# First two unit pairs multiply a split x, the norm factor moves to the eviction, and the taps are dealt out anew: conv and retention trunk on one core

## The chip, the core and the metric

The kernel runs on one core of a Trainium2 chip. The metric is the time of one execution on the device in microseconds (us). All products are made on TensorE (PE); VectorE (DVE), ScalarE (ACT) and GpSimd (POOL) do the elementwise work, SyncE (SP) issues most of the loads.

## The reference, cut to what matters

Sequence 512, model width 1024, inner width 2048, float32, two layers and a last norm:

```python
h = rms_norm(x, conv_norm)                  # x * r * g, r = 1/sqrt(mean(x^2) + eps) for each token
a, b, z = split(h @ w_in, 3)                # w_in: 1024 x 6144
u = a * sigmoid(b)
c = causal_depthwise_conv(u, 31 taps) + dw_b
y = silu(layer_norm(c)) * silu(z)
x = x + y @ w_out
x = x + retention(rms_norm(x, ret_norm))    # q, k, v, gate projections, rotary, chunks of 128
out = rms_norm(x, final_norm)
```

r is one number for each token, so (x * g * r) @ w is ((x * g) @ w) * r: the factor can be put in before the products or at their eviction.

## The kernel before, in words

Everything is held with channels on the 128 partitions and the 512 tokens along the free axis. x is 8 tiles of 128x512, u and c are 16 tiles each. Weights come from HBM in 64 pairs of units; a unit is 128x1024, which is 8 blocks of 128x128 for one output tile (two units make one u tile: unit 2j gives a, unit 2j+1 gives b).

Where a product has to be exact to float32, both factors are split into a high part (rounded to the type fp32r) and the rest, and three products are added: `mm3` (L231 to L235) does hi*hi, hi*lo, lo*hi. One unit is 24 such products. The pair 0 is the exception: `raw0` and `xg` (x times the norm's weight) are unsplit float32 and are multiplied in one pass each at L328 (16 products, for which the trace shows two records each).

**The start.** Ten products of zeros keep TensorE warm (`keep_warm`, L133). x and pair 0 are loaded, ACT squares each x tile (L295), DVE sums them up (L299), a product with ones gives the token sums (L288), `rsqrt` on DVE gives r (L250 to L267), and a product with the identity spreads it over the partitions as R1 (L273), in the middle of the products of pair 0. Then `h_tile` (L671) makes h = xg * R1 in PSUM (L674), ACT rounds it to its high part (L675), and `h_lo` (L677) makes the rest on DVE. `split_pair` (L681) splits pairs 1 and 2, with the low part on POOL. Pair 1 is multiplied at L735 to L742, first with all high parts of the weights, then with the low ones; its products wait for the h tiles one by one. From unit 4 on `unit_mm` (L745) runs one unit after the other. Here the high and low parts come from ACT (L198, L202: 1.9 us for a pair each) and from a DMA that POOL issues and that adds raw onto the negated high part (`dma_lo`, L204).

**The taps.** A u tile takes 31 taps of 128x512 for its c tile, 496 taps in all. Four ways take them: the first tap of a tile on ACT (`first_tap`, L373), a tap on DVE (L521: c = u shifted * w + c, in PSUM), a tap as a product on ACT and an add on POOL (`product` L432, `pool_add` L441), and a pair step: two products of tiles 2n and 2n+1 on ACT, added by one DMA of 512 KB that POOL issues (`pair_step` L408, `pair_add` L422).

**What sets the order.** From the start of this stage to the end of the layer norm the order on each engine is written out by hand (manual schedule): a planner in the kernel keeps a clock with five lines (`Clock`, L77) and in `fill` (L554) always emits the step that can start first. `pool_tile` (L536) picks the tile for POOL's next add: the tile next to be taken up by DVE or the one behind it, up to `POOL_CAP` taps, and not the first if `RATE` says that it would be late. `pair_of` (L397) lets a pair take a pair step if both its u tiles exist, none of its adds waits on POOL, it has done fewer than `STEPS`, its tiles lie behind the one next to be taken up, and one of two sum buffers is free (`room`, L393). Between pair steps the planner lets the DMA land and then 7 us pass (`QWAIT`), so an add that follows is put some 10.1 us (1.55 + 1.46 + 0.1 + 7.0) behind the DMA's issue. Only the pairs in `PAIRS` are asked.

```python
STEPS = 4
PAIRS = (2, 3, 4, 5)
...
        p = n // 2 + 1 + n % 2
...
            neg_hi(p)
            fill(it.done[f"wneg{p}"])
            dma_lo(p)
...
        prev = (prev or ()) + (unit_mm(n),)
        fill(it.now[PE_])
```

**The end of the stage.** Units 46 and 47 are held back (`HOLD`, L794); `work` (L800) puts their products, three at a time, between the products of the layer norm's sums (`tail`, L828), and where they have run out, products of zeros into `idle` (L811). Then follow the norm's factors, y and the output projection (L936 to L959), and the retention layer, whose order the scheduler sets.

## Time and profile before

| | us |
|---|---|
| median of 3 runs | 805.14 (802.46 to 807.92) |
| the profiled execution | 804.36 |
| its span, first to last instruction | 802.4 |
| mean granted TensorE clock | 0.993 |

The profile is of one execution; the span leaves out 2.0 us around it. A row of a timeline gives the start, the time from its start to its end (for several instructions merged, from the first start to the last end), the engine, the line of the kernel, the operation, what it writes and reads, and in brackets how long the engine had been idle before it and what ended that. An instruction begins before the one ahead of it has ended, so a merged row divided by its count is the step from one to the next.

### The profile page before, as it was taken

The page shows a single profiled execution, that of the slowest core. Times are in us where ns is not written, and L with a number is a line of the kernel's source. Part 1 is how long each engine was busy: PE and PEld are TensorE (multiplying, and loading weights), DVE is VectorE, ACT ScalarE, POOL GpSimd, SP SyncE. Part 2 cuts the span into 40 slices and gives each one's busy share as a digit, 9 for nine tenths or more (in the row PEclk, how much of TensorE's full clock was granted, in tenths as well). Part 3 has the DMA queues.
Part 4 walks back from the last instruction along what each step waited for, and adds up shares of the span by engine and source line. Part 5 has one row for each costly group of instructions (what it writes and reads, how often), then busy time and mean ns, then how long its engine had stood idle before and what let it go on. Part 6 is the DMA issues. An engine that isn't in the chain of part 4 may idle for free.

```text
span 802.4 us, 9733 instructions
## 1 busy us (share of the span) xinstructions
PE 789.1 (98%) x3681; PEld 651.7 (81%) x3681; DVE 576.8 (72%) x855; ACT 422.2 (53%) x561; POOL 365.8 (46%) x286
## 2 busy tenths in 40 slices
PE   8999999999999999999999999999999999999995
PEld 3588888888888888888888888888888888888895
DVE  4899999999999948899574576486586467542434
ACT  3589889888998727543233413423424424332421
POOL 0578999989999848720330322340340120000300
PEclk9999999999999999999999999999999999999998
DMA  7367857897798734433213212112122212222103
GB/s 276 124 174 176 210 164 167 211 238 176 199 232 214 182 108 145 171 105 106 105 54 128 81 53 105 53 54 105 52 69 96 99 53 105 105 105 105 53 1 105
DMA packets 18958, 101.58 MB, mean 127 GB/s; under 512 B 2272, under 2 KB 4320, under 8 KB 8032
## 3 DMA queue, kind: packets, MB, share of 16 engines
q1 hardware_dynamic: 14448, 74.73, 26.6%
q0 software_dynamic: 4032, 25.69, 15.8%
q8 instruction: 29, 0.48, 0.2%
q10 hardware_dynamic: 432, 0.54, 0.2%
q14 instruction: 17, 0.14, 0.0%
HBM read 73.17 MB, written 2.10 MB: 94 GB/s over the span
## 4 chain that ended last, share of the span: by engine, by line
PE 95%; DVE 2%; DMA 2%; ACT 1%; issue 0%; SPq 0%; DVEq 0%; ACTq 0%
PE mm L233 28%; PE mm L235 27%; PE mm L234 27%; PE mm L959 2%; PE mm L957 2%; PE mm L958 2%; DMA g<-xT 1%; PE dsum L288 1%; PE mm L328 1%; PE st L288 1%; PE acc L235 1%; PE acc L234 1%; PE acc L233 1%; PE mm L742 0%; PE st L647 0%; DMA nrm<-norms 0%
## 5 line engine op out<-in xcount | busy, mean ns | idle before, releaser
L233 PE MATMUL mm<-g,whi 128*128 128x512 f32 (+1 forms) x832 | 319.8, 385 | 0.0
L234 PE MATMUL mm<-g,whi 128*128 128x512 f32 (+1 forms) x832 | 317.5, 382 | 0.0
L235 PE MATMUL mm<-g,wlo 128*128 128x512 f32 (+1 forms) x832 | 316.8, 381 | 0.0
L521 DVE SCALAR_TENSOR_TENSOR acc<-u,cpar,acc 128x512 f32<-128x512 f32 x324 | 220.8, 753 | 4.7 <-ACT acc L473 3.0
L299 POOL TENSOR_TENSOR accp<-accp,prod 128x512 f32<-128x512 f32 x142 | 190.6, 1383 | 17.2 <-ACT prod L436 10.7
L233 PEld LDWEIGHTS mm<-g,whi 128*128 128x128 f32 x832 | 156.5, 188 | 30.3 <-issue 0.7
L234 PEld LDWEIGHTS mm<-g,whi 128*128 128x128 f32 x832 | 156.5, 188 | 30.1 <-issue 1.0
L235 PEld LDWEIGHTS mm<-g,wlo 128*128 128x128 f32 x832 | 156.4, 188 | 29.9
L187 ACT CAST whi<-raw 128x1024 fp32r<-128x1024 f32 x80 | 80.7, 1050 | 111.3 <-PE mm L234 69.2
L192 DVE TENSOR_TENSOR wlo<-raw,whi 128x1024 fp32r<-128x1024 f32 x70 | 94.5, 1384 | 41.3 <-ACT whi L187 41.3
L299 POOL TENSOR_TENSOR g<-g,g 128x512 f32<-128x512 f32 x23 | 35.5, 1544 | 179.9 <-ACT g L295 171.4
L436 ACT ACTIVATE prod<-u,cpar 128x512 f32<-128x512 f32 x142 | 97.3, 719 | 20.1 <-POOL accp L299 20.0
L1045 POOL TENSOR_TENSOR g<-g,g 128x512 f32<-128x512 f32 x8 | 10.4, 1294 | 142.7 <-DVE g L1043 142.7
L228 DVE TENSOR_TENSOR g<-g,g 128x512 fp32r<-128x512 f32 x36 | 29.0, 820 | 35.7 <-ACT g L227 32.2
L227 ACT CAST g<-g 128x512 fp32r<-128x512 f32 x36 | 22.4, 623 | 60.0 <-POOL g L1045 27.8
L234 PE MATMUL mm<-wlo,g 128*128 128x512 f32 x128 | 49.8, 389 | 0.0
L235 PE MATMUL mm<-whi,g 128*128 128x512 f32 x128 | 49.6, 389 | 0.0
L233 PE MATMUL mm<-whi,g 128*128 128x512 f32 x128 | 49.3, 389 | 0.0
L198 ACT ACTIVATE wlo<-raw 128x2048 fp32r<-128x2048 f32 x21 | 40.1, 1909 | 0.0
L202 ACT CAST whi<-raw 128x2048 fp32r<-128x2048 f32 x21 | 40.0, 1904 | 0.0
L1112 POOL TENSOR_TENSOR o<-o,g 128x512 f32<-128x512 f32 x16 | 27.5, 1747 | 18.2 <-DVE g L267 18.2
L192 POOL TENSOR_TENSOR wlo<-raw,whi 128x1024 fp32r<-128x1024 f32 x10 | 24.3, 2428 | 14.9 <-ACT whi L187 14.9
(207 smaller groups left out, 960.9 us busy)
## 6 DMA issues: line engine op xcount, KB each, us to landing
raw<-wpack SPq DMA_DIRECT2D x63, 1024.0 KB, 4.8
wlo<-raw POOLq DMA_DIRECT2D x21, 1024.0 KB, 8.2
g<-xT SPq DMA_DIRECT2D x16, 256.0 KB, 6.3
q<-q POOLq DMA_DIRECT2D x6, 512.0 KB, 8.0
out_dram<-xo SPq DMA_DIRECT2D x6, 256.0 KB, 2.5
dec<-decay SPq DMA_DIRECT2D x1, 1280.0 KB, 7.5
raw<-wpack ACTq DMA_DIRECT2D x2, 256.0 KB, 5.5
raw<-wpack SPq DMA_DIRECT2D x2, 256.0 KB, 5.6
```

Of the source, the lines that this page charges most:

```text
L187: it.run(ACT_, 0.95, lambda: nc.scalar.copy(his[p][:, i, :], raws[p][:, i, :]), f"whi{n}")
L192: it.run(e, c, lambda: eng.tensor_tensor(out=lo, in0=raws[n // 2][:, n % 2, :], in1=hi.bitcast(F32), op=ALU.subtract), f"wlo{n}", [f"whi{n}"])
L198: it.run(ACT_, 1.8, lambda: nc.scalar.activation(los[p], raws[p], AF.Copy, scale=-1.0), f"wneg{p}")
L202: it.run(ACT_, 1.8, lambda: nc.scalar.copy(his[p], raws[p]), f"whi{p}", deps)
L228: (eng or nc.vector).tensor_tensor(out=lo, in0=src, in1=hi.bitcast(F32), op=ALU.subtract)
L233: nc.tensor.matmul(o, a[0], b[0], start=first, stop=False)
L234: nc.tensor.matmul(o, a[0], b[1], start=False, stop=False)
L235: nc.tensor.matmul(o, a[1], b[0], start=False, stop=last)
L299: eng.tensor_tensor(out=a, in0=a, in1=b, op=ALU.add)
L436: at = it.run(ACT_, 0.61, lambda: nc.scalar.activation(p, u_sb[j][:, w:w + S], AF.Copy, scale=cpar[:, j, w:w + 1]), at=add_end[n_prod[0]])
L521: it.run(DVE_, cost, lambda: nc.vector.scalar_tensor_tensor(out=c_sb[j] if last else acc, in0=u_sb[j][:, w:w + S], scalar=cpar[:, j, w:w + 1],
L1112: nc.gpsimd.tensor_tensor(out=t, in0=t, in1=RO, op=ALU.mult)
```

## The change

- Pair 0 and pair 1 are multiplied with a split of x times the norm's weight (`xs`), not of h. Pair 0 is split too and goes through `mm3`. The factor r comes in when the two pairs are evicted: tile 0 as before with R1, tile 1 with two more multiplications on DVE (`bR1`, `sR1`).
- The order of the start is another: ACT makes the high parts of x and of pair 0 tile by tile, DVE the low parts, POOL adds four of the squares, two products of zeros are put after each of six tiles. The token sums stand ahead of the last tile's products, the spreading of r stands after two tiles of pair 1.
- raw0 lies in the ring of the raw pairs (2 buffers), its parts in the rings whi and wlo; ACT's table for the sigmoid is loaded at the very start.
- h is made from x, the weight and R1 in one step; the first four tiles lie in SBUF with the low part on POOL, the others in PSUM with the low part on DVE.
- The constants of the taps are set anew: STEPS, PAIRS, POOL_CAP, LEAD, RATE.

```diff
-STEPS = 4
-PAIRS = (2, 3, 4, 5)
+STEPS = 5
+PAIRS = (1, 2, 3, 4, 5, 6)
...
-POOL_CAP = 16
-LEAD = 8
-RATE = 1.6
+POOL_CAP = 13
+LEAD = 3
+RATE = 1.81
...
+HPOOL = 4
...
-    raw0 = ring.tile([P, KD, 2, P], F32, tag="wlo", bufs=3, name="raw0")
+    raw0, hi0, lo0 = [ring.tile([P, KD, 2, P], dt, tag=tag, bufs=n, name=tag + "0")
+                      for tag, dt, n in (("raw", F32, 2), ("whi", F32R, 2), ("wlo", F32R, 3))]
     w0 = wpack[0].rearrange("p a (b c d) -> p (a b) c d", c=2, d=P)
     x_sb = [G() for _ in range(KD)]
     for k in range(0, KD, 2):
         (nc.scalar if k < 4 else nc.sync).dma_start(out=raw0[:, k:k + 2], in_=w0[:, k:k + 2])
-        if k < 4:
-            for i in range(4):
-                nc.sync.dma_start(out=x_sb[2 * k + i], in_=xT[:, 2 * k + i, :])
+        for i in range(2):
+            nc.sync.dma_start(out=x_sb[k + i], in_=xT[:, k + i, :])
+
+    nc.scalar.activation(sp.tile([P, 1], F32, name="tbl"), wz[:, 0:1], AF.Sigmoid)
...
-    xg, sq = [], []
+    xs, sq = [], []
     pa, pb = MM(), MM()
-    r1 = R1 = None
+    o_st = ST(NT)
+
+    def pair0(k):
+        for c, o in enumerate((pa, pb)):
+            mm3(o, (hi0[:, k, c, :], lo0[:, k, c, :]), xs[k], k == 0, k == KD - 1)
+
     for k in range(KD):
-        t = G()
-        nc.vector.tensor_scalar(out=t, in0=x_sb[k], scalar1=nrm[:, 0, k:k + 1], scalar2=None, op0=ALU.mult)
-        xg.append(t)
+        xh, xl = G(F32R), G(F32R)
+        g = nrm[:, 0, k:k + 1]
+        nc.scalar.activation(xh, x_sb[k], AF.Copy, scale=g)
+        if k % 2 == 0:
+            nc.scalar.copy(hi0[:, k:k + 2], raw0[:, k:k + 2])
+        nc.vector.scalar_tensor_tensor(out=xl, in0=x_sb[k], scalar=g, in1=xh.bitcast(F32), op0=ALU.mult,
+                                       op1=ALU.subtract)
+        if k % 2 == 0:
+            nc.vector.tensor_tensor(out=lo0[:, k:k + 2], in0=raw0[:, k:k + 2], in1=hi0[:, k:k + 2].bitcast(F32),
+                                    op=ALU.subtract)
         sq.append(square(x_sb[k]))
-        if k:
-            tadd(nc.vector, sq[0], sq[k])
-
-    nc.scalar.activation(sp.tile([P, 1], F32, name="tbl"), nrm[:, 0, 0:1], AF.Sigmoid)
-    for i in range(2 * KD):
-        k, c = divmod(i, 2)
-        nc.tensor.matmul((pa, pb)[c], raw0[:, k, c, :], xg[k], start=k == 0, stop=k == KD - 1)
-        if i == SUMS_AT:
-            r1 = rsqrt(token_sums([sq[0]]), 1.0 / 1024.0)
-        if i == BCAST_AT:
-            R1, R1_sb = ST(), G()
-            bcast_mm(r1, R1)
-            nc.scalar.copy(R1_sb, R1)
-    it.now = [21.7, 17.2, 17.2, 17.2, 21.0]
-    it.done["R1"] = 17.2
-    it.done["pab"] = 21.7
+        xs.append((xh, xl))
+        if 0 < k < 5:
+            tadd(nc.gpsimd, sq[0], sq[k])
+        if k > 5:
+            tadd(nc.vector, sq[5], sq[k])
+        if k == KD - 1:
+            token_sums([sq[0]], o_st, True, False)
+            token_sums([sq[5]], o_st, False, True)
+        pair0(k)
+        if k < KD - 2:
+            keep_warm(2)
+    r1 = rsqrt(o_st, 1.0 / 1024.0)
+    it.now = [17.2, 15.0, 18.0, 15.0, 20.0]
+    it.done["pab"] = 17.2
...
-        if j:
+        if j == 1:
+            it.run(DVE_, 0.66, lambda: nc.vector.tensor_tensor(out=sg, in0=pb, in1=R1_sb, op=ALU.mult), "bR1", ["mm3"])
+            it.run(ACT_, 0.5, lambda: nc.scalar.activation(sg, sg, AF.Sigmoid), "sg1", ["bR1"])
+            fill(it.done["sg1"])
+            it.run(DVE_, 0.66, lambda: nc.vector.tensor_tensor(out=sg, in0=sg, in1=R1, op=ALU.mult), "sR1", ["sg1"])
+        else:
...
     h_s = []
-    h_ps = []
+    h_sb = []
 
     def h_tile(k):
         h_s.append((G(F32R), G(F32R)))
-        h_ps.append(ACC() if k % 3 < 2 else MM())
-        it.run(DVE_, 0.64, lambda: nc.vector.tensor_tensor(out=h_ps[k], in0=xg[k], in1=R1, op=ALU.mult), f"h{k}", ["R1"])
-        it.run(ACT_, 0.52, lambda: nc.scalar.copy(h_s[k][0], h_ps[k]), f"hh{k}", [f"h{k}"])
+        h_sb.append(G() if k < HPOOL else ACC())
+        it.run(DVE_, 0.66, lambda: nc.vector.scalar_tensor_tensor(
+            out=h_sb[k], in0=x_sb[k], scalar=nrm[:, 0, k:k + 1], in1=R1, op0=ALU.mult, op1=ALU.mult), f"h{k}", ["R1"])
+        it.run(ACT_, 0.52, lambda: nc.scalar.copy(h_s[k][0], h_sb[k]), f"hh{k}", [f"h{k}"])
 
     def h_lo(k):
-        it.run(DVE_, 0.64, lambda: nc.vector.tensor_tensor(out=h_s[k][1], in0=h_ps[k], in1=h_s[k][0].bitcast(F32),
-                                                           op=ALU.subtract), f"hl{k}", [f"hh{k}"])
+        e, c, eng = (POOL_, 1.35, nc.gpsimd) if k < HPOOL else (DVE_, 0.66, nc.vector)
+        it.run(e, c, lambda: eng.tensor_tensor(out=h_s[k][1], in0=h_sb[k], in1=h_s[k][0].bitcast(F32),
+                                               op=ALU.subtract), f"hl{k}", [f"hh{k}"])
...
     os_ = [MM(), MM()]
     u0, sg0 = u_ring[0], cp.tile([P, S], F32, tag="sg", bufs=1, name="sg0")
+    R1, R1_sb = ST(), G()
+    list(split_pair(1, 16.5))
+    load(3)
+    ws = [unit(n) for n in (2, 3)]
+    for k in range(KD):
+        for c in range(2):
+            a = ws[c][0][:, k * P:(k + 1) * P]
+
+            def hi_mms():
+                nc.tensor.matmul(os_[c], a, xs[k][0], start=k == 0, stop=False)
+                nc.tensor.matmul(os_[c], a, xs[k][1], start=False, stop=False)
+
+            it.run(PE_, 0.45, hi_mms, None, ["whi1"])
+        if k == 1:
+            it.run(PE_, 0.95, lambda: bcast_mm(r1, R1), "R1", at=18.1)
+    for k in range(KD):
+        for c in range(2):
+            it.run(PE_, 0.227, lambda: nc.tensor.matmul(os_[c], ws[c][1][:, k * P:(k + 1) * P], xs[k][0], start=False,
+                                                       stop=k == KD - 1), f"mm{2 + c}", ["wlo1"])
+    it.run(ACT_, 0.52, lambda: nc.scalar.copy(R1_sb, R1), "R1_sb", ["R1"])
     h_tile(0)
-    pair = split_pair(1, 17.5)
-    next(pair)
+    pair = split_pair(2, 20.5)
+    it.run(DVE_, 0.66, lambda: nc.vector.tensor_tensor(out=sg0, in0=pb, in1=R1_sb, op=ALU.mult), "bR", ["pab", "R1_sb"])
+    h_lo(0)
     h_tile(1)
-    h_lo(0)
-    next(pair)
+    it.run(ACT_, 0.52, lambda: nc.scalar.activation(sg0, sg0, AF.Sigmoid), "sg", ["bR"])
+    h_lo(1)
     h_tile(2)
-    h_lo(1)
-    list(pair)
-    load(3)
-    pair = split_pair(2, 21.4)
-    it.run(DVE_, 0.66, lambda: nc.vector.tensor_tensor(out=sg0, in0=pb, in1=R1_sb, op=ALU.mult), "bR", ["pab"])
-    it.run(ACT_, 0.52, lambda: nc.scalar.activation(sg0, sg0, AF.Sigmoid), "sg", ["bR"])
-    h_lo(2)
-    h_tile(3)
     it.run(DVE_, 0.66, lambda: nc.vector.tensor_tensor(out=sg0, in0=sg0, in1=R1, op=ALU.mult), "sR0", ["sg"])
     it.run(DVE_, 0.66, lambda: nc.vector.tensor_tensor(out=u0[:, PADW:], in0=pa, in1=sg0, op=ALU.mult), "u0", ["sR0"])
     u_sb[0] = u0
+    next(pair)
+    h_tile(3)
+    next(pair)
+    h_lo(2)
+    h_tile(4)
     h_lo(3)
-    next(pair)
-    h_tile(4)
     first_tap(0)
-    next(pair)
+    list(pair)
     h_tile(5)
     h_lo(4)
-    list(pair)
     h_tile(6)
     h_lo(5)
     h_tile(7)
     h_lo(6)
     h_lo(7)
-    it.now[ACT_] = max(it.now[ACT_], 31.5)
+    fill(27.0)
+    it.now[ACT_] = max(it.now[ACT_], 27.0)
     neg_hi(3)
+    fill(it.done["wneg3"])
     dma_lo(3)
     load(4)
-    ws = [unit(n) for n in (2, 3)]
-    for k in range(KD):
-        for c in range(2):
-            a = ws[c][0][:, k * P:(k + 1) * P]
-
-            def hi_mms():
-                nc.tensor.matmul(os_[c], a, h_s[k][0], start=k == 0, stop=False)
-                nc.tensor.matmul(os_[c], a, h_s[k][1], start=False, stop=False)
-
-            it.run(PE_, 0.45, hi_mms, None, [f"hl{k}"])
-    for k in range(KD):
-        for c in range(2):
-            it.run(PE_, 0.227, lambda: nc.tensor.matmul(os_[c], ws[c][1][:, k * P:(k + 1) * P], h_s[k][0], start=False,
-                                                       stop=k == KD - 1), f"mm{2 + c}", ["wlo1"])
+    it.now[PE_] = max(it.now[PE_], it.done["hl7"] - 4.7)
```

## Rows read from the trace of the kernel before

**Rows 1.** The page: the chain that ended last, by engine.
```profile
PE 95%; DVE 2%; DMA 2%; ACT 1%; issue 0%; SPq 0%; DVEq 0%; ACTq 0%
```

**Rows 2.** Stretches: PE, PEld, DVE, ACT, POOL busy; clock; DMA share; GB/s.
```profile
33.00:36.70 3.70, 3.48 (x8) 2.83 (x9) 3.49 (x7) 2.40 (x2) 1.60 (x2) 0.54 0.30 75
41.30:279.50 238.20, 238.20 (x1087) 197.11 (x1086) 233.17 (x350) 209.65 (x260) 220.83 (x181) 1.00 0.78 195
...
150.00:200.00 50.00, 50.00 (x242) 42.03 (x241) 49.10 (x75) 42.41 (x52) 46.47 (x40) 1.00 0.90 210
```

**Rows 3.** Timeline of PE, start: zeros, token sums, spreading; zeros at the end.
```profile
1.32 4.45 PE L137 MATMUL acc<-wz 128*128 128x512 bf16 x10 [1.32 <-POOL wz L131]
...
14.65 1.02 PE L288 MATMUL st<-ones,g 128*128 128x1 f32 x8 [1.82 <-DVE g L299]
...
19.89 1.05 PE L273 MATMUL st<-ident,rs 128*128 128x128 f32 x8
...
792.27 2.32 PE L137 MATMUL acc<-wz 128*128 128x512 bf16 x10
```

**Rows 4.** Chain in order of time (start, us, what): last products of pair 1.
```profile
37.60 3.65 PE mm L742 x16
```

**Rows 5.** Groups by line and form on DVE, 340 to 400: line, operation, count, busy, mean ns.
```profile
L975 DVE SCALAR_TENSOR_TENSOR g<-g,nrm,g 128x512 fp32r<-128x512 f32 x8 | 11.0, 1395 | 0.0
```

**Rows 6.** Timeline of DVE, POOL, ACT: h tiles, splits, first taps, a DMA issue, taps.
```profile
21.60 1.29 DVE L674 TENSOR_TENSOR acc<-g,st 128x512 f32<-128x512 f32 x2 [3.73 <-ACT g L334]
...
32.04 2.38 POOL L689 TENSOR_TENSOR wlo<-raw,whi 128x1024 fp32r<-128x1024 f32 x1 [0.83 <-ACT whi L687]
...
34.28 1.92 ACT L198 ACTIVATE wlo<-raw 128x2048 fp32r<-128x2048 f32 x1
...
35.03 0.75 DVE L517 TENSOR_SCALAR acc<-u,cpar 128x512 f32<-128x512 f32 x1
...
42.59 2.67 POOL L299 TENSOR_TENSOR accp<-accp,prod 128x512 f32<-128x512 f32 x2 [5.06 <-ACT prod L436]
...
48.98 0.88 POOL L206 DMA_DIRECT2D wlo<-raw  x1
49.59 11.10 POOL L299 TENSOR_TENSOR accp<-accp,prod 128x512 f32<-128x512 f32 x8
...
229.80 26.38 DVE L521 SCALAR_TENSOR_TENSOR acc<-u,cpar,acc 128x512 f32<-128x512 f32 x39
```

**Rows 7.** Timeline of ACT: u tiles 7, 9, 11, 13 (L661), take-up of 5, 7, 9 (L473).
```profile
110.34 0.58 ACT L661 ACTIVATE sg<-mm 128x512 f32<-128x512 f32 x1
...
117.90 0.57 ACT L473 COPY acc<-accp 128x512 f32<-128x512 f32 x1
...
132.44 0.58 ACT L661 ACTIVATE sg<-mm 128x512 f32<-128x512 f32 x1
...
141.25 0.59 ACT L473 COPY acc<-accp 128x512 f32<-128x512 f32 x1
...
153.71 0.60 ACT L661 ACTIVATE sg<-mm 128x512 f32<-128x512 f32 x1 [0.55 <-PE mm L235]
...
170.47 0.59 ACT L473 COPY acc<-accp 128x512 f32<-128x512 f32 x1 [1.61 <-POOL accp L299]
...
178.82 0.58 ACT L661 ACTIVATE sg<-mm 128x512 f32<-128x512 f32 x1
```

**Rows 8.** DMA issues: target, queue, count, KB each, median us from issue to landing.
```profile
raw<-wpack SPq DMA_DIRECT2D x63, 1024.0 KB, 4.8
...
accp<-prod POOLq DMA_DIRECT2D x1, 512.0 KB, 6.9
```

**Rows 9.** The instructions of L206 (raw added onto the low part by DMA), landing.
```profile
DMA to landing us min/median/max: 6.9/8.2/11.5
```

**Rows 10.** Timeline of DVE and PE: the last sum of a tile, its token sums.
```profile
278.77 0.69 DVE L500 TENSOR_TENSOR g<-accp,acc 128x512 f32<-128x512 f32 x1 [0.18 <-POOL accp L299]
...
283.44 0.95 PE L288 MATMUL dsum<-ones,g 128*128 128x1 f32 x8
```

More of the change, by code (lines that the diff above doesn't have):

```diff
@@ L50 @@
 WARM = 10
-SUMS_AT = 7
-BCAST_AT = 10
 DMA_LAG = 1.55
```

## The prediction

> **What bounds the kernel now.** I read the page's chain first: it runs 95% of the span through PE [rows 1]. Whoever stops there expects each us saved on PE to come off the time. The second view is the busy time by stretch. Between 41.3 and 279.5 us PE is busy all 238.2 us, but DVE is busy 233.2, POOL 220.8 and ACT 209.7 [rows 2]: in the taps four engines are full at once, and PE is only the one that is a little fuller. The third view is the timeline at both ends of that stage. At its start DVE's first tap begins at 35.03 and POOL's first add at 42.59 [rows 6], while PE ends pair 1 at 37.60 + 3.65 = 41.25 [rows 4]. At its end DVE has the last sum at 278.77 + 0.69 = 279.46, and PE comes to its token sums at 283.44, 4.0 later [rows 10]. So PE binds, with some 3 us between it and the taps. A change that makes PE much earlier at the start passes the end of this stage on to the taps.
>
> **Part 1: the start on PE.** The change takes away 16 one-pass float32 products and the waits of pair 1 for the h tiles, and adds 48 fp32r products for pair 0. A product of that form takes 3.65 / 16 = 0.228 [rows 4], one of zeros 2.32 / 10 = 0.23, a tile's token sums 1.02, the spreading of r some 1.0 [rows 3]. The zeros at the front end at 1.32 + 4.45 = 5.8 [rows 3]. Then pair 0 takes 48 x 0.228 = 10.9, the zeros put in between 12 x 0.23 = 2.8, two tiles' sums 2.0: 21.5. To it I add 0.7 for one low part of x that comes late: an instruction of the same form and size takes 1.395 beside POOL adds [rows 5], where one of DVE's h instructions takes 0.69 [rows 6]; four adds of squares run on POOL then, but PE has 1.37 + 0.46 of work for a tile, more than the 1.395, so I count one of the four. Pair 0 ends at 22.2. Eight products of pair 1 (1.8) bring PE to 24.0, the spreading to 25.0 (R1), the other 40 (9.1) to 34.1. Against 41.25 PE is **7.1 us earlier**. Bounds: no collision 33.4; all four collisions (2.8), zeros at 4.45 / 10 each as at the front (2.6 more) and one stretch like 33.0 to 36.7, where 0.54 of the clock is granted (3.7 x 0.46 = 1.7 lost) [rows 2], 34.1 + 2.1 + 2.6 + 1.7 = 40.5. So PE gains 0.8 to 7.9.
>
> By the Trainium skill (SBUF — State Buffer, Who interferes with whom) a VectorE instruction with two inputs in SBUF and a GpSimd instruction that reads SBUF shut each other out for the whole length of one of them; the new low parts of x and of pair 0 are such instructions. The trace agrees in kind: twice 0.69 in rows 5. By the rule each of the four adds costs up to its whole 1.39, all four on the path 5.6 instead of 0.7, and as all that follows waits for R1 the sum below would be 4.9 worse, 804.2; by the row it would be 2.1 worse with all four, 801.4.
>
> **Part 2: the start of the taps.** From R1 at 25.0 DVE has 15 instructions (8 h, 4 low parts, 3 for u0) at 1.29 / 2 = 0.645 [rows 6], 9.7, and perhaps 0.5 of waits for ACT's rounding: first tap at 35.2, against 35.03. Two more multiplications for u1 take 1.3, so DVE is **1.5 late**, though PE is early. POOL starts on the h tiles at about 26.5, and has four low parts at 11.10 / 8 = 1.39 and two splits at 2.38 [rows 6]: 36.9. Only then is that raw buffer free for pair 4, which lands 4.8 later [rows 8]; ACT negates it in 1.92 ahead of its first products (0.7): first add at 44.3, against 42.59, **1.7 late**. What PE gains hides neither. Bounds: no wait of ACT and products put ahead of pair 4, 0.5 early; all of part 1's delay on R1, 6 late. What POOL takes over of the h tiles (four at 1.39) is in this sum; the table load, the ring for raw0 and the order of loads lie beside the zeros and the splits, at nothing; should pair 2's raw (which now waits for raw0's last split) come late, unit 4 would wait, and PE has the room for it.
>
> **Part 3: who takes the taps.** DVE takes 39 / 26.38 = 1.478 taps a us and POOL 8 / 11.10 = 0.721, together 2.20 [rows 6]. Starting 1.5 and 1.7 late costs (1.5 x 1.478 + 1.7 x 0.721) / 2.20 = **1.6 us**. A pair step takes 2 taps and costs POOL the issue, 49.59 - 48.98 = 0.61 [rows 6], so 0.44 of a tap: 1.56 taps, or 0.71 us off the end. Before there is one step [rows 8], since its window is short: pair n opens when u(2n+1) exists and closes when tile 2n-1 is taken up. For pairs 3, 4, 5 this is 110.3 to 117.9, 132.4 to 141.3, 153.7 to 170.5 [rows 7]. With the u tiles 7.1 earlier and the take-ups where they are, they are 15, 16 and 24 us; a step holds its pair for some 12 us (two products, the issue, 10.1 planned behind it), so 1, 1 and 2 steps. Pair 6 is new: u13 at 178.8 - 7.1 = 171.7 [rows 7], a buffer free from 170.5, POOL busy with tiles 10 and 11: all five. Pair 1 never opens, since tile 2 is the next to be taken up from the time that DVE has tiles 0 and 1. Nine steps, 8 more: 8 x 0.71 = **5.7 us**. ACT makes 12.5 more products at about 0.65, 8 us of its 28 idle [rows 2]. Bounds: none more to 12 more, 0 to 8.5. POOL_CAP, RATE and LEAD only move POOL's work between tiles; I count them at nothing, between POOL's idle time of 238.2 - 220.8 = 17.4 gone (17.4 x 0.721 / 2.20 = 5.7 better) and doubled (5.7 worse).
>
> **Part 4: the end.** Of the 3 us that PE lags there I take 1.0 as won, since PE then has products of zeros in hand; bounds 0 and 3.0.
>
> **The sum.** 5.7 - 1.6 + 1.0 = 5.1, which is less than PE's 7.1; the other 2 us go into 9 products of zeros. The profiled execution took 804.4 (span 802.4 and 2.0 around it; the median of the runs is 0.8 above): **799.3 us**.
>
> **Rivals.** First, the taps keep up and all of PE's gain arrives: 804.4 - 7.1 = 797.3. For it: five pairs that may step; it needs 11 more steps, not 8. Against: POOL stands still while it waits for a tile under a step. Second, the change doesn't do what it says: steps stay at one, because a POOL add of the pair's first tile always comes ahead; then 804.4 + 1.6 - 1.0 = 805.0, and 7 us of zeros on PE. For it: one step in 33 us of open windows [rows 7]. Third, on the other side, the DMAs of the steps land late. The 16 DMA engines are at 0.90 from 150 to 200 [rows 2], where pair 6 would step. An add on POOL is put 10.1 behind the issue; one landed after 6.9 [rows 8], the larger ones of L206 after up to 11.5 [rows 9]. Each us beyond 10.1 stops POOL for nine steps, 9 x 0.33 = 3.0 us of the end: from a landing of 11.8 on the gain is gone, at 13 it is 8.7 - 5.1 = 3.6 slower, 808.0.
>
> **How the numbers follow.** Forecast 0.50 (own range 797 to 802), first rival 0.20, second 0.20, third 0.10. The range leaves out the far end of the third and a little below PE's bound: 795.5 to 806.0. A measurement of this kernel tells about 1% from no change, 8.0 us: below 796.3 lie half of the first rival, whose bound is 7.9, and 0.02 of the forecast, 0.12; above 812.4 lies less than half of the third, 0.04; within, 0.84.
>
> **What would show it.** Right: pair 1 ends near 34; the first tap is at 35 to 36; nine 512 KB additions into the sums; some nine products of zeros at L811's place; DVE's last sum about 4 to 5 earlier. Wrong: no zeros there (then PE still binds), steps at one or two, 512 KB landings above 12, or PE ends pair 1 after 38.

## The result, and the profile after

| | before | after |
|---|---|---|
| median of the runs, us | 804.06 | 815.97 (815.11 to 818.91) |
| ratio | 1 | 1.0147 (95%: 1.0101 to 1.0194) |
| profiled execution, span | 804.36, 802.4 | 816.22, 814.4 |
| spreading of r (PE), start | 19.89 | 31.61 |
| first tap (DVE) / first add (POOL) | 35.03 / 42.59 | 44.91 / 50.93 |
| DVE's last sum, end | 279.46 | 291.31 |

The change costs 12 us. The forecast was 799.3, so the sign was wrong and the time lies outside the range. The page's chain answers to [rows 1]:

```profile
PE 76%; DVE 9%; ACT 4%; POOL 4%; DMA 3%; issue 3%; ACTq 0%; DVEq 0%; SPq 0%; POOLq 0%
```

PE had 95%. A fifth of the chain now runs through DVE, ACT, POOL and DMAs. The timelines show where it leaves PE. They answer to [rows 3], [rows 4], [rows 6] and [rows 10]; the spreading of r is L274, the first products of low parts of x L329, the additions of squares L300, the split of pair 1 L707:

```profile
8.55 1.32 POOL L300 TENSOR_TENSOR g<-g,g 128x512 f32<-128x512 f32 x1 [6.06 <-ACT g L296]
9.11 1.32 DVE L329 SCALAR_TENSOR_TENSOR g<-g,nrm,g 128x512 fp32r<-128x512 f32 x1 [0.38 <-ACT g L326]
10.27 4.73 POOL L300 TENSOR_TENSOR g<-g,g 128x512 f32<-128x512 f32 x3 [0.39 <-ACT g L296]
10.35 1.79 DVE L332 TENSOR_TENSOR wlo<-raw,whi 128x512 fp32r<-128x512 f32 x1
12.06 3.48 DVE L329 SCALAR_TENSOR_TENSOR g<-g,nrm,g 128x512 fp32r<-128x512 f32 x2
...
16.07 1.40 DVE L329 SCALAR_TENSOR_TENSOR g<-g,nrm,g 128x512 fp32r<-128x512 f32 x2
...
17.85 5.24 POOL L707 TENSOR_TENSOR wlo<-raw,whi 128x1024 fp32r<-128x1024 f32 x2 [2.85 <-ACT whi L705]
18.00 2.88 DVE L300 TENSOR_TENSOR g<-g,g 128x512 f32<-128x512 f32 x1
20.80 2.83 DVE L329 SCALAR_TENSOR_TENSOR g<-g,nrm,g 128x512 fp32r<-128x512 f32 x1
23.56 0.68 DVE L300 TENSOR_TENSOR g<-g,g 128x512 f32<-128x512 f32 x1
24.29 1.87 PE L289 MATMUL st<-ones,g 128*128 128x1 f32 x8 [2.29 <-DVE g L300]
31.61 1.05 PE L274 MATMUL st<-ident,rs 128*128 128x128 f32 x8
33.32 0.75 DVE L690 SCALAR_TENSOR_TENSOR g<-g,nrm,st 128x512 f32<-128x512 f32 x1 [4.98 <-ACT g L732]
...
37.98 3.79 PE L730 MATMUL mm<-g,wlo 128*128 128x512 f32 x16
...
44.91 0.75 DVE L528 TENSOR_SCALAR acc<-u,cpar 128x512 f32<-128x512 f32 x1
...
46.41 1.01 POOL L207 DMA_DIRECT2D wlo<-raw  x1 [1.07 <-ACT wlo L199]
50.93 2.66 POOL L300 TENSOR_TENSOR accp<-accp,prod 128x512 f32<-128x512 f32 x2 [3.51 <-ACT prod L447]
55.48 0.50 PE L236 MATMUL mm<-g,wlo 128*128 128x512 f32 x1 [2.39 <-DMA wlo<-raw]
...
85.19 1.67 PE L658 MATMUL st<-g,onesm 128*128 128x512 f32 x2 [2.66 <-DVE g L511]
...
269.21 1.26 PE L289 MATMUL dsum<-ones,g 128*128 128x1 f32 x8 [1.53 <-DVE g L511]
...
290.62 0.69 DVE L511 TENSOR_TENSOR g<-accp,acc 128x512 f32<-128x512 f32 x1
```

Read the durations on DVE first. The same addition takes 0.68 at 23.56 and 2.88 at 18.00; the low part of an x tile takes 0.70 at 16.07 and 2.83 at 20.80. The long ones all lie beside a POOL instruction that reads SBUF, and each ends shortly after that does. Beside the four additions of squares DVE loses 1.32 - 0.70 + 1.79 - 0.69 + 3.48 - 1.40 = 3.8 us, beside the split of pair 1 2.88 - 0.68 + 2.83 - 0.70 = 4.3. PE stands 2.29 us for the second token sums, and then the stretches, with the columns of [rows 2], show what follows:

```profile
20.00:25.30 5.30, 3.01 (x19) 2.70 (x17) 4.24 (x3) 0.00 (x0) 3.09 (x2) 0.89 0.59 212
25.30:31.00 5.70, 5.70 (x17) 4.64 (x17) 1.81 (x11) 0.00 (x0) 0.00 (x0) 0.50 0.36 148
...
44.91:291.31 246.40, 239.56 (x1069) 196.08 (x1068) 235.68 (x356) 213.22 (x264) 218.69 (x182) 0.99 0.84 204
```

For 5.7 us PE is busy at 0.50 of its clock, the lower level of 1.2 GHz. Pair 1 ends at 37.98 + 3.79 = 41.8, no earlier than the 41.25 of before. The last row is the taps' stage, from the first tap to the end of the last sum: 246.4 us, against 244.4 before, and PE is no longer busy all through it.

Before, PE waits nowhere in this stage. In after it stands three times: 2.39 for a low part that comes by DMA, 2.66 for DVE's sum of the first tile (85.19), and 1.53 for that of a late one (269.21). Behind the last two its clock falls: it is 0.70 and 0.87 in the two stretches of 4 us from 84 to 92, and 0.74 and 0.83 in those from 268 to 276. I laid the products of units 4 to 47 of both timelines beside each other, number by number: after's PE is 0.5 us behind before's at first, 3.2 behind the first of these waits, 7.7 from 96 us on, 8.6 just ahead of the third, and 12.0 at the end of unit 47. That is the whole of the 12 us. DVE's last sum is not itself what the end waits for: PE comes to the token sums of that tile at 296.16, 4.9 later (4.0 before).

The groups in that stage (the last columns are the idle time ahead and who ended it), of after:

```profile
L532 DVE SCALAR_TENSOR_TENSOR acc<-u,cpar,acc 128x512 f32<-128x512 f32 x320 | 216.3, 750 | 8.9 <-ACT acc L484 5.7 <-ACT acc L481 2.6
L300 POOL TENSOR_TENSOR accp<-accp,prod 128x512 f32<-128x512 f32 x136 | 184.9, 1421 | 9.7 <-ACT prod L447 4.1
...
L199 ACT ACTIVATE wlo<-raw 128x2048 fp32r<-128x2048 f32 x21 | 40.1, 1907 | 5.1 <-DMA raw<-wpack 5.1
L207 POOL DMA_DIRECT2D wlo<-raw x21 | 19.3, 920 | 13.6 <-ACT wlo L199 11.4 <-PE mm L236 1.9
```

and of before:

```profile
L521 DVE SCALAR_TENSOR_TENSOR acc<-u,cpar,acc 128x512 f32<-128x512 f32 x324 | 220.8, 753 | 4.7 <-ACT acc L473 3.0
L299 POOL TENSOR_TENSOR accp<-accp,prod 128x512 f32<-128x512 f32 x142 | 190.6, 1383 | 17.2 <-ACT prod L436 10.7
...
L198 ACT ACTIVATE wlo<-raw 128x2048 fp32r<-128x2048 f32 x21 | 40.1, 1909 | 0.0
L206 POOL DMA_DIRECT2D wlo<-raw x21 | 18.8, 893 | 5.3 <-ACT wlo L198 4.8 <-issue 0.2
```

DVE has only 4 taps fewer, POOL 6 adds fewer, and DVE waits longer. The pair steps did come (answering to [rows 8]):

```profile
accp<-prod POOLq DMA_DIRECT2D x6, 512.0 KB, 6.8
```

### The profile page after: what moved, and what is told of

It is laid out like the page before. It is cut to its first block, busy times and chain, and to the rows that moved or that the text cites. A ratio compares the mean times of both kernels' runs of the same rounds, so it can differ in the third digit from the quotient of the medians.

```text
span 814.4 us, 9820 instructions
## 1 busy us (share of the span) xinstructions
PE 794.5 (98%) x3716; PEld 659.9 (81%) x3716; DVE 582.0 (71%) x848; ACT 429.5 (53%) x576; POOL 373.7 (46%) x293
## 4 chain that ended last, share of the span: by engine, by line
PE 76%; DVE 9%; ACT 4%; POOL 4%; DMA 3%; issue 3%; ACTq 0%; DVEq 0%; SPq 0%; POOLq 0%
PE mm L234 22%; PE mm L235 22%; PE mm L236 22%; DVE acc L532 5%; POOL accp L300 3%; DMA raw<-wpack 2%; PE mm L981 2%; PE mm L979 2%; PE mm L980 2%; ACT wlo L199 1%; DMA wlo<-raw 1%; PE st L289 1%; PE acc L236 1%; PE acc L235 1%; PE acc L234 1%
## 5 line engine op out<-in xcount | busy, mean ns | idle before, releaser
L234 PE MATMUL mm<-g,whi 128*128 128x512 f32 (+1 forms) x848 | 330.6, 390 | 1.1 <-ACT whi L328 1.1
L236 PE MATMUL mm<-g,wlo 128*128 128x512 f32 (+1 forms) x848 | 325.1, 384 | 2.4 <-DMA wlo<-raw 2.4
L235 PE MATMUL mm<-g,whi 128*128 128x512 f32 (+1 forms) x848 | 325.7, 384 | 0.0
L532 DVE SCALAR_TENSOR_TENSOR acc<-u,cpar,acc 128x512 f32<-128x512 f32 x320 | 216.3, 750 | 8.9 <-ACT acc L484 5.7
L300 POOL TENSOR_TENSOR accp<-accp,prod 128x512 f32<-128x512 f32 x136 | 184.9, 1421 | 9.7 <-ACT prod L447 4.1
L234 PEld LDWEIGHTS mm<-g,whi 128*128 128x128 f32 x848 | 161.0, 190 | 33.8 <-ACT whi L328 2.0
L236 PEld LDWEIGHTS mm<-g,wlo 128*128 128x128 f32 x848 | 160.5, 189 | 34.1 <-DMA wlo<-raw 2.8
L235 PEld LDWEIGHTS mm<-g,whi 128*128 128x128 f32 x848 | 160.9, 190 | 30.9 <-issue 1.2
L300 POOL TENSOR_TENSOR g<-g,g 128x512 f32<-128x512 f32 x27 | 41.4, 1535 | 186.5 <-ACT g L296 177.8
L447 ACT ACTIVATE prod<-u,cpar 128x512 f32<-128x512 f32 x136 | 93.1, 715 | 17.1 <-POOL accp L300 16.9
L1067 POOL TENSOR_TENSOR g<-g,g 128x512 f32<-128x512 f32 x8 | 10.3, 1292 | 142.7 <-DVE g L1065 142.7
```

Source lines behind the costliest of these rows:

```text
L234: nc.tensor.matmul(o, a[0], b[0], start=first, stop=False)
L235: nc.tensor.matmul(o, a[0], b[1], start=False, stop=False)
L236: nc.tensor.matmul(o, a[1], b[0], start=False, stop=last)
L300: eng.tensor_tensor(out=a, in0=a, in1=b, op=ALU.add)
L447: at = it.run(ACT_, 0.61, lambda: nc.scalar.activation(p, u_sb[j][:, w:w + S], AF.Copy, scale=cpar[:, j, w:w + 1]), at=add_end[n_prod[0]])
L532: it.run(DVE_, cost, lambda: nc.vector.scalar_tensor_tensor(out=c_sb[j] if last else acc, in0=u_sb[j][:, w:w + S], scalar=cpar[:, j, w:w + 1],
```

## The experiments

In all tables "stage" is the time from the first tap to the end of DVE's last sum, and "idle" is that less DVE's busy time in it; all are read from the one profiled execution of each kernel. Before has 244.4 with 5.3 idle, after 246.4 with 10.7. One profile says only so much: the five kernels that have after's code as far as the spreading of r start it between 30.16 and 31.61, the seven that have before's between 19.89 and 21.59.

### The five constants

Four kernels separate the constants from the start: before with all five new ones, with the two of the pair steps, with the three of POOL's share, and after with the old ones.

```diff
-STEPS = 4
-PAIRS = (2, 3, 4, 5)
+STEPS = 5
+PAIRS = (1, 2, 3, 4, 5, 6)
-POOL_CAP = 16
-LEAD = 8
-RATE = 1.6
+POOL_CAP = 13
+LEAD = 3
+RATE = 1.81
```

> The kernel before with only the five constants of the taps set anew (STEPS, PAIRS, POOL_CAP, LEAD, RATE). Theory 1 (the loss comes from the start: low parts of x on DVE are shut out by POOL's split of pair 1, so that R1, the h tiles and the first tap come 8 to 10 us late): the constants do no harm; some pair steps more than the one of before, 0.71 us each, so 800 to 804 where before takes 804. Theory 2 (the constants deal the taps out worse: POOL stands still under pair steps, DVE waits at take-ups): 808 or more, with more idle time of POOL and DVE in the taps.

> The kernel before with the two constants of the pair steps alone (STEPS 5, PAIRS 1 to 6); the three of POOL's share stay old. Theory 1 (a pair step gains its 1.56 taps, and what took the gain away in the run with all five constants is the new POOL share: cap 13, lead 3, rate 1.81): some 5 to 6 pair additions of 512 KB, landing near 7, last sum of DVE 2 to 4 us ahead of before's 278.8, time 800 to 803, ratio 0.995 to 0.999. Rival (the steps themselves give nothing, because POOL waits for the sums that are under way and ACT makes the products in place of the low parts): 5 to 6 additions, last sum at 279 to 282, ratio 1.000 to 1.005, POOL idle time in the taps 3 to 6 us above before's.

> The kernel before with the three constants of POOL's share alone (cap 13, lead 3, rate 1.81); the pair constants stay old. Theory 1 (this is what took away the gain of the steps): POOL loses adds and DVE takes more, last sum 2 to 4 us later than 278.8, time 806 to 809, ratio 1.002 to 1.006. Rival (the steps themselves give nothing): within 0.2% of before with 1 or 2 pair additions, last sum 278 to 280.

> The changed kernel with the five old constants. Theory 1 (the start is late): the first tap of DVE stays at 45, one or two pair steps instead of six, so 816 to 820. Theory 2 (the constants): 804 to 808, although the start is as late.

| kernel | ratio (95%) | pair steps | POOL adds | last sum ends | stage, idle |
|---|---|---|---|---|---|
| before, all five | 1.0036 (1.0006 to 1.0065) | 6 | 133 | 281.4 | 246.2, 8.6 |
| before, pair steps | 0.9995 (0.9975 to 1.0015) | 5 | 136 | 279.4 | 242.7, 5.4 |
| before, POOL's share | 0.9997 (0.9972 to 1.0022) | 2 | 137 | 282.6 | 247.3, 6.6 |
| after, old constants | 1.0083 (1.0055 to 1.0112) | 3 | 134 | 294.4 | 250.7, 9.4 |

Five more pair steps take 10 taps, but POOL makes 9 adds fewer with them (133 for 142), 1.8 for a step where I had put 0.44. Some of these 9 belong to POOL's share: set anew alone it makes 5 adds fewer with one step more. With the pair constants alone it is 6 adds for four steps, 1.5. There a step leaves 0.5 of its 2 taps, where I had counted 1.56, and the gain does not show in the time. (The stage with the pair constants alone is short because its start was 1.7 later; the last sum is before's.) Neither half of the constants alone moves the time; together they cost 0.4% (median 807.2, between the two forecasts). On after's start the median with the old ones is lower, 811.9, between the two forecasts as well. Its last sum is 3.1 later than after's and its profiled execution 5.2 shorter: 514.5 us lie behind the last sum instead of 523.1, since some 50 products that after's PE makes behind that sum stand ahead of it here. So a later last sum is not always a longer time.

### What makes r late

Three kernels take one cause each out of after's start: the split of pair 1 on POOL (its low part comes by DMA), the sums of squares on POOL and DVE (PE sums all eight tiles), and the gap on PE (12 products of zeros between the two token sums).

```diff
-    list(split_pair(1, 16.5))
+    neg_hi(1)
+    dma_lo(1)
+    new_hi(1)
```

```diff
-        if 0 < k < 5:
-            tadd(nc.gpsimd, sq[0], sq[k])
-        if k > 5:
-            tadd(nc.vector, sq[5], sq[k])
...
+            token_sums([sq[k]], o_st, k == 0, False)
```

```diff
             token_sums([sq[0]], o_st, True, False)
+            keep_warm(12)
             token_sums([sq[5]], o_st, False, True)
```

> The changed kernel, but the low part of pair 1 is made by a DMA that adds raw onto the negated high part, as for the later pairs, so that POOL computes nothing between the adds of squares (over at 15.0) and the h tiles. Theory 1 (DVE instructions with two SBUF inputs wait for POOL's split): the sum of squares 6 and the last low part of x take 0.7 each instead of 2.8, the second token sums come at 21 to 22 instead of 24.3, without a gap that lowers the clock, R1 at 26 to 28 instead of 32.6, the time at 807 to 811. Rival (something else holds DVE at 18 to 23.6, the arrival of x or the ACT parts): both stay at 2.8 and the time at 814 to 817.

> The changed kernel, but the squares are not added up on POOL and DVE: PE makes the token sums of each of the eight square tiles, in place of the twelve products of zeros. The order of all that follows is untouched. Theory 1: with no POOL adds beside the low parts of x and no sums of squares in DVE's queue ahead of the last low part, that one is done at 17 to 18, before POOL's first split of pair 1, R1 comes at 25 to 27 instead of 32.6, the first tap at 37 to 39 instead of 44.9, and the time is 806 to 810. Theory 2: the start is not what counts, 814 to 817.

> The changed kernel with twelve more products of zeros between the two groups of token sums, where PE stands idle from 22.0 to 24.3 and then has half the clock until 31. Theory 1 with the shut-out as the main cost: the clock is the smaller part, R1 about 2.5 us earlier, 812 to 814. Rival: the fallen clock is the main cost, R1 5 us or more earlier, 810 or less.

| kernel | ratio (95%) | spreading | first tap | last sum ends | stage, idle |
|---|---|---|---|---|---|
| no split on POOL | 1.0087 (1.0057 to 1.0117) | 25.33 | 38.63 | 285.7 | 247.0, 11.4 |
| sums on PE | 1.0113 (1.0078 to 1.0148) | 27.32 | 40.57 | 286.4 | 245.9, 10.3 |
| zeros in the gap | 1.0097 (1.0069 to 1.0125) | 27.77 | 41.08 | 286.6 | 245.5, 9.8 |

Without the split the three instructions of DVE that closed the sums are short again; its timeline:

```profile
17.45 0.68 DVE L300 TENSOR_TENSOR g<-g,g 128x512 f32<-128x512 f32 x1
18.05 0.74 DVE L329 SCALAR_TENSOR_TENSOR g<-g,nrm,g 128x512 fp32r<-128x512 f32 x1
18.72 0.68 DVE L300 TENSOR_TENSOR g<-g,g 128x512 f32<-128x512 f32 x1
```

With zeros in the gap PE keeps its full clock in the stretches where after had 0.89 and 0.50:

```profile
20.00:25.30 5.30, 5.30 (x34) 3.60 (x33) 4.05 (x7) 0.00 (x0) 2.33 (x1) 1.00 0.63 223
25.30:31.00 5.70, 5.70 (x31) 4.82 (x30) 2.76 (x11) 1.21 (x2) 0.04 (x1) 1.00 0.23 93
```

So the split beside DVE's last instructions is the largest cause (6.3 us of r; 4.8 against the earliest of the five kernels with after's start), and the gap with the half clock behind it is worth 3.8 (2.4). They overlap: the split makes the gap. The medians are 809.9, 813.2 and 812.5, as forecast for the first and the third and above the forecast for the second; the intervals overlap, so which of the three saves most time is not shown. In each of the three the first tap comes 13.3 after the spreading's start, and the last sum is earlier with it. But none has a stage as short as before's.

### A start without any of it, and with r still earlier

The "clear" start adds the squares on DVE behind the low parts, takes pair 1's low part from the DMA, and spreads r after the first tile of pair 1. The "early" start lets ACT square x ahead of splitting it, sums each tile on PE at once, and spreads r in the middle of pair 0. Each ran with the new and the old constants.

```diff
-            tadd(nc.gpsimd, sq[0], sq[k])
+        if k > 1:
+            tadd(nc.vector, sq[0], sq[k - 1])
...
-        if k == 1:
+        if k == 0:
             it.run(PE_, 0.95, lambda: bcast_mm(r1, R1), "R1", at=18.1)
```

```diff
+    def sum_(k):
+        token_sums([sq[k]], o_st, k == 0, k == KD - 1)
...
+    bcast_mm(r1, R1)
+    for fn, k in ((pair0, 3), (xh_, 4), (hi_, 4), (xl_, 4), (lo_, 4), (pair0, 4), (xh_, 5), (xl_, 5), (pair0, 5),
```

> The changed kernel with a start that has no POOL computation beside the low parts of x: squares are added on DVE behind the low parts, pair 1's low part comes by DMA, one product of zeros instead of two after each of six tiles, r is spread after one tile of pair 1 instead of two. Constants new. Theory 1 (the end follows the first tap one for one: 804.5 span for a first tap at 35.0 with these constants): R1 at 22 to 24, first tap at 34 to 37, time 804 to 808. Rival (the taps lose by themselves with a faster PE, whatever the start): above 810.

> The same clear start with the five old constants. Theory 1: first tap at 34 to 37, and by the run with the old constants (808.9 span at a first tap of 43.7) 799 to 803, so level with the kernel before or a little faster. Rival (constants do not matter once the start is clear): the same time as with the new ones within 2 us.

> The kernel after with the token sums brought forward: ACT squares the tiles of x ahead of splitting them, PE takes the sums of each tile of squares by themselves instead of sums made on GpSimd and DVE, r is spread in the middle of pair 0, pair 1's low part comes from the DMA, and the h tiles stand ahead of the two splits of tile 0's eviction; the new constants stay. Theory 1 (the end of the taps follows the first tap, and that follows R1): spreading at 17 to 20, first tap at 30 to 33, pair 1 ends at 35 to 38, last sum 277 to 281, time 799 to 805, ratio 0.994 to 1.001. Rival (the taps' stage has lost 2 to 3 us of its own by the change): first tap at 30 to 33 too, but the last sum 280 to 283 and the time 803 to 807. Third (PE now waits, since the splits come behind the squares): pair 1 ends after 39 and the first tap after 36.

> The same start with the five old constants. Theory 1: the first tap within 0.5 us of the run with the new ones, 1 to 3 pair additions, time within 3 us of it. If the new constants are what costs the taps their speed: 2 to 4 us faster than the run with the new ones, 798 to 802; if the pair steps pay once the u tiles come early: 2 to 4 us slower than that.

| kernel | ratio (95%) | spreading | first tap | last sum ends | stage, idle |
|---|---|---|---|---|---|
| clear, new constants | 1.0043 (1.0017 to 1.0068) | 24.05 | 37.53 | 284.9 | 247.4, 11.8 |
| clear, old | 1.0073 (1.0047 to 1.0099) | 23.44 | 36.76 | 286.0 | 249.3, 8.0 |
| early, new | 1.0079 (1.0047 to 1.0110) | 20.96 | 36.11 | 285.9 | 249.8, 11.2 |
| early, old | 1.0097 (1.0059 to 1.0135) | 24.75 | 39.92 | 294.1 | 254.2, 8.3 |

The clear start wins back 1% of the 1.5%; its median of 807.7 was forecast with the new constants, the 809.4 with the old ones was not (799 to 803). The early start was a miss, by its third theory: r was spread at 20.96, but I had put ACT's work for pairs 1 and 3 among the h tiles, DVE waited 3.4 for it, and the first tap came at 36.1. With r a us later than before's, the first tap only 1.1 and POOL's first add (45.35) 2.8 later, its last sum is still 6.4 later. So r is not all; the stage itself loses.

### The late start by itself

Before, with idle work on DVE (14 multiplications) and POOL (7 additions) ahead of the taps; nothing else is moved.

```diff
     h_lo(7)
+    for i in range(14):
+        nc.vector.tensor_tensor(out=scr[0], in0=R1, in1=R1_sb, op=ALU.mult)
+    for i in range(7):
+        nc.gpsimd.tensor_tensor(out=scr[1], in0=x_sb[0], in1=x_sb[1], op=ALU.add)
```

> The kernel before with 14 idle multiplications on DVE (about 0.68 each, 9.5 us) and 7 idle additions on GpSimd (about 1.35 each, 9.4 us) behind the h tiles, ahead of the first tap; TensorE's products of pair 1 and the written order stay as they are. Theory 1 (what the change costs is the late start of the taps, nearly one for one, since the rates of the taps share it out: (9.5 x 1.478 + 9.4 x 0.721) / 2.20 = 9.5): first tap at 44 to 45, POOL's first add at 51 to 52, last sum 287 to 290, time 812 to 816, ratio 1.009 to 1.014. Rival (a late start alone is half made up, because other work is waiting in the taps, and the change loses the rest inside them): last sum before 285, time 807 to 811.

The ratio is 1.0127 (1.0090 to 1.0164), as forecast. Timelines of POOL, DVE and PE:

```profile
44.69 2.93 POOL L299 TENSOR_TENSOR accp<-accp,prod 128x512 f32<-128x512 f32 x2
45.10 0.74 DVE L517 TENSOR_SCALAR acc<-u,cpar 128x512 f32<-128x512 f32 x1
...
54.40 2.67 POOL L299 TENSOR_TENSOR accp<-accp,prod 128x512 f32<-128x512 f32 x2 [6.77 <-ACT prod L436]
64.61 0.50 PE L233 MATMUL mm<-g,whi 128*128 128x512 f32 x1 [2.84 <-ACT whi L202]
79.80 1.33 PE L647 MATMUL st<-g,onesm 128*128 128x512 f32 x2 [3.99 <-DVE g L500]
...
287.09 0.69 DVE L500 TENSOR_TENSOR g<-accp,acc 128x512 f32<-128x512 f32 x1 [0.22 <-POOL accp L299]
```

DVE's first tap is 10.07 later than before's, the last sum 8.32 and the end 7.7. POOL is late too: its idle additions hold its first issue of a low part back from 36.52 to 43.93, and while its first two adds are only 2.1 later, its third is at 54.40 (46.33 before, 54.18 in after). The stage is 242.7, 1.75 shorter, with DVE idle for 3.8:

```profile
45.10:287.78 242.68, 235.85 (x1067) 194.09 (x1066) 238.88 (x358) 205.61 (x255) 220.55 (x181) 0.99 0.78 194
```

The rows of PE show where the late start is paid: PE waits 2.84 for a high part that ACT makes late and 3.99 for the sum of the first tile, and its clock is 0.57 from 80 to 84. Product by product it is 7.7 behind before's from 85 us on, and 7.7 at the end of unit 47; it doesn't wait again, and 89% of the page's chain is PE's. So the late start is paid once, at the first tile, and from there on PE binds again. After is 7.7 behind at that place too. Its other 4.3 us come later, 3.4 of them at the wait of 269.21, and by the stages it is 3.7 longer than this kernel. The times alone do not part the two kernels: their intervals overlap.

### What the taps lose

In after, as in all its relatives, POOL stands longer ahead of its issues of low parts. Two of them lie 7.2 us apart there (46.41 and 53.57), and the load of weights issued at 55.5 lands late, as does one issued at 158.7 behind issues 7.9 apart. The two loads, issue to landing, in after:

```profile
DMA to landing us min/median/max: 10.0/10.0/10.0
...
DMA to landing us min/median/max: 11.4/11.4/11.4
```

The median is 4.8. For both, ACT waits (2.76 and 2.29), and POOL behind it. Close issues are not the only cause: in before the load issued at 173.7 took 10.0 as well, behind issues 10.5 apart.

The first tile's sum is also late by the written order. It begins 39.5 us behind the first tap in after, 34.3 before, because DVE has 51 taps and four u tiles ahead of it instead of 47 and three, and the two multiplications for u1. With the old constants it is 39.3, so it comes with the new start. PE's product for this sum lies a unit later in its order as well, so what that costs is not shown.

Three kernels put the issue 3 us later in the written order (after, the clear start, before with the new constants), one keeps the issues of after 10.3 us apart.

```diff
-            fill(it.done[f"wneg{p}"])
+            fill(it.done[f"wneg{p}"] + 3.0)
             dma_lo(p)
```

```diff
-            fill(it.done[f"wneg{p}"])
+            fill(max(it.done[f"wneg{p}"], lo_at[0] + 10.3))
             dma_lo(p)
+            lo_at[0] = it.now[POOL_]
```

> The kernel after with the DMA issue of each low part put 3 us later in the written order of GpSimd, so that the additions come ahead of it. Theory 1 (GpSimd's standing in front of this issue costs the taps their 2 us): its idle time ahead of the issue falls from 13.6 us to below 6, the stretch from the first tap to the last sum from 246.4 to 244 or 245, time 813 to 815. Rival (the standing is only a sign that GpSimd has nothing else to do): the idle time moves to its additions, the stretch stays at 246 to 248, time 815 to 818.

> The same 3 us in the kernel with the clear start (h_clear_new). Theory 1: idle time ahead of the issue below 6 us instead of 14.1, stretch 244 to 246 instead of 247.4, time 804 to 806.5. Rival: stretch 247 to 249, time 807 to 809.

> The same 3 us in the kernel before with the five new constants (a_consts_only). Theory 1: idle time ahead of the issue below 6 us instead of 15.4, so POOL makes 3 to 6 more additions, the stretch 243 to 245 instead of 246.2, time 802 to 805, ratio 0.997 to 1.001. Rival: stretch 246 to 248, ratio 1.003 to 1.006.

> The kernel after, with the DMA issues of the low parts kept at least 10.3 us apart in the written order. Theory 1 (the collision of two low-part DMAs with a load is what the taps lose): no load of weights in the taps lands later than 8 us at the start (10.0 in after for the one issued at 55.5) nor near 158; ACT does not wait for a load ahead of a negated part; idle time of GpSimd ahead of these issues under 7 us instead of 13.6; the stretch from first tap to last sum 243 to 245.5 instead of 246.4; time 812 to 814.5, ratio 1.009 to 1.013. Rival (the pair steps are the cause: ACT and GpSimd cannot keep the order with six of them): the loads land early and the stretch is still 246 to 249, time 815 to 818.

| kernel | ratio (95%) | idle of POOL ahead of the issue | stage, idle of DVE |
|---|---|---|---|
| after, 3 us | 1.0159 (1.0109 to 1.0209) | 6.2 (13.6) | 249.0, 12.8 |
| clear, 3 us | 1.0047 (1.0022 to 1.0073) | 6.8 (14.1) | 245.7, 9.5 |
| before, new constants, 3 us | 1.0039 (1.0018 to 1.0060) | 5.0 (15.4) | 246.9, 8.3 |
| after, 10.3 us apart | 1.0193 (1.0156 to 1.0230) | 1.1 (13.6) | 250.3, 13.5 |

In brackets the kernel without the edit. None of the four ratios is clear of that of the kernel without the edit. With 3 us the idle time fell as theory 1 says, or nearly, but the stage did so only with the clear start, and that profile is of the fastest of eleven executions (802.3, median 808.7). After with 3 us has a median of 814.0, as theory 1 says, and a stage of 249.0, as it doesn't. POOL's groups of after with 3 us, and then of after with the issues apart POOL's groups, PE's wait for low parts (total, times, longest) and a row of PE's timeline:

```profile
L301 POOL TENSOR_TENSOR accp<-accp,prod 128x512 f32<-128x512 f32 x132 | 178.8, 1418 | 24.9 <-ACT prod L448 19.7
L208 POOL DMA_DIRECT2D wlo<-raw x21 | 19.5, 929 | 6.2 <-ACT wlo L200 6.2
```

```profile
L301 POOL TENSOR_TENSOR accp<-accp,prod 128x512 f32<-128x512 f32 x135 | 184.7, 1435 | 26.8 <-ACT prod L448 21.6
...
L208 POOL DMA_DIRECT2D wlo<-raw x21 | 20.3, 965 | 1.1 <-ACT wlo L200 1.1
...
PE mm L237 <- DMA wlo<-raw: 10.9, 7, 3.4
...
81.84 1.10 PE L659 MATMUL st<-g,onesm 128*128 128x512 f32 x2 [0.50 <-DVE g L512]
```

The standing moved from the issues to the additions: POOL waits for ACT in one place or in the other. With the issues apart these two collisions are gone (all loads issued from 43.9 to 144.6 land within 5.8, and in the taps ACT waits for none before 165). What that is worth the run does not tell, since the edit holds up PE: it waits for low parts in seven places, 10.9 in all, where after waits once, 2.39. Ahead of most of these waits there is a gain: PE waits only 0.50 for the first tile's sum, and behind it is 2.7 behind before's PE, where after is 7.7, though it began unit 4 only 1.4 earlier. By this the first collision may have cost after some 3.6 us (7.7 - 2.7 - 1.4, an estimate from two profiles), and later waits eat it up. In its profile the clock is also 0.72 in the 30 us behind the last sum, where after has 1.00, so its end at 826.1 is not the stage's alone. So what the taps lose stays open in part: the first collision, the order ahead of the first tile's sum and the waits for ACT (ACT is busy only 213 of 246 us) lie on top of each other, and no run here takes them apart.

### The other direction

Before, with the low parts of h tiles 4 to 7 made on POOL between its two splits, so that DVE comes to the taps earlier.

```diff
-        h_ps.append(ACC() if k % 3 < 2 else MM())
+        h_ps.append(G() if k >= KD - HPOOL else ACC() if k % 3 < 2 else MM())
...
+        e, c, eng = (POOL_, 1.35, nc.gpsimd) if k >= KD - HPOOL else (DVE_, 0.64, nc.vector)
```

> The kernel before with the low parts of h tiles 4 to 7 made on GpSimd from SBUF, between its splits of pair 1 and pair 2; DVE goes from its last h tile straight to the taps. Everything else is before's. Theory 1 (the end follows the start of the taps on DVE): DVE has 4 x 0.69 less ahead of its first tap, 32 to 33 instead of 35.03; the last sum 276 to 278 instead of 278.77, time 801 to 803.5, ratio 0.996 to 0.9995. Rival (PE binds, or GpSimd's issue of pair 3's low part, some 4 us later, stops unit 6): pair 1 ends after 41.3 or PE waits at unit 6, last sum 279 or later, ratio 1.000 to 1.004.

The ratio is 1.0063 (1.0043 to 1.0084), longer than either theory said. Its timelines:

```profile
31.31 5.03 POOL L680 TENSOR_TENSOR g<-g,g 128x512 fp32r<-128x512 f32 x4 [1.72 <-ACT g L676]
32.30 0.74 DVE L518 TENSOR_SCALAR acc<-u,cpar 128x512 f32<-128x512 f32 x1
...
36.30 4.76 POOL L691 TENSOR_TENSOR wlo<-raw,whi 128x1024 fp32r<-128x1024 f32 x2
...
282.95 0.69 DVE L501 TENSOR_TENSOR g<-accp,acc 128x512 f32<-128x512 f32 x1 [0.50 <-POOL accp L300]
```

The first tap is 2.7 earlier, as forecast, and the last sum 4.2 later. POOL's splits of pair 2, which ended at 34.4 [rows 6], end at 41.1; the first two issues of low parts lie 8.8 apart, and POOL stands 14.4 ahead of these issues, for 5.3. So an early DVE gained nothing here, with POOL's queue and the loads behind it later; which of these costs the 4.2 is not shown. Making the low parts of h all on DVE in after (HPOOL = 0) was no gain either:

> The changed kernel with HPOOL = 0: all h tiles in PSUM, all low parts on DVE. Theory 1: h in SBUF with low parts on POOL is not what costs; DVE has four instructions of 0.69 more and waits for PSUM buffers, so the first tap comes 2 to 4 us later and the time is 815 to 820. Rival (the POOL low parts hold up the h tiles): the first tap earlier than 44 and the time below 813.

Its ratio is 1.0173 (1.0145 to 1.0200) and its median 817.0, as forecast; the first tap is at 45.85, 0.9 later and not 2 to 4, POOL's first add at 53.66, and POOL makes 123 adds beside nine pair steps. No kernel of the study is shown to be faster than before.

## Why the prediction was wrong

**What bounds the kernel** was right: PE waits nowhere in before's taps, and the taps have little in hand. The 3 us that I read from the end [rows 10] hold at the other end of the stage too: PE comes to the first tile's sum at 73.73, 3.7 behind DVE (70.02).

**Part 1 failed, in its collision term and in R1 at 25.0.** I charged 0.7 for one addition of squares beside one low part. DVE lost 3.8 beside the additions, more than my bound of 2.8, and 4.3 more beside the split of pair 1. The latter was not in the working at all: the change moves this split from behind R1 to ahead of it, where DVE still had three instructions to go until the token sums, and I looked for collisions only where additions of squares stood. The Trainium skill (SBUF — State Buffer, Who interferes with whom), which I weighed for the four additions alone, says that each shuts the other out for a whole instruction; after's 2.88 and 2.83 beside a split of some 2.6 bear it out, and the run without the split gives 0.68 and 0.74. The gap that follows is 2.29 long and costs PE half of its clock for 5.7 us, 2.85 lost, where I had 1.7 as a bound. R1 was there at 31.61 + 1.05 = 32.7, 7.7 late, and pair 1 ended at 41.8, beyond my bound of 40.5.

**Part 2** took R1's error over and added its own: from R1 to the first tap 12.2, not 10.2. DVE waits for ACT's copy of R1 before the first h tile (33.32) and for its rounding between them. So the first tap was at 44.91, not 35.2. My bound for the first tap was 6 late; it was 9.9. The price was wrong in kind as well: I had shared a late start out by the rates of the taps, but the run with a late start on DVE and POOL shows it paid by PE, which waits at the first tile: 7.7 us of span for a first tap 10.07 late, and after is 7.7 behind at that tile too.

**Part 3's 5.7 us** did not come. Six steps, not nine, landed in 6.8, so the third rival did not come in. In work they paid: DVE is busy 235.7 in the stage where the kernel with the late start has 238.9, though it has two multiplications more. But DVE is idle 10.7 instead of 3.8. I had priced a step by POOL's issue, 0.44 of an add; the runs lost 1.2 to 1.8 adds for each, some of them to POOL's new share. I counted ACT's 28 us of idle time [rows 2] as cover. In a queue with an order it may not be free for work put ahead of something that others wait for, and DVE does wait more for ACT (8.9 ahead of its taps, 4.7 before), but that this is the cause is argued and not shown. POOL_CAP, RATE and LEAD, which I counted at nothing, moved nothing alone (0.9997).

**Part 4's 1.0** fell with the rest: no products of zeros stand at the end. None of the rivals came in. The sum as measured by its steps: the last sum was forecast at 279.46 - 5.7 + 1.6 = 275.4 and came at 291.3, 15.9 later; 9.7 of it is the first tap (44.91 - 35.2), 6.2 the stage (246.4 - 240.2). In the time PE's waits show the same two parts: 7.7 by the first tile, 4.3 behind it. The first goes back to the start: at the same place PE is some 3.6 behind without the split and 0.5 with the clear start. Of the second the cause stays open.
